# Two-layer hybrid backbone: the short convolution's projections in pieces of six products inside the first segment's attention

## The chip, the cores and the metric

One core of one Trainium2 chip runs the whole program in one launch. The metric is the device time of one execution in microseconds; lower is better. Everything is computed in 32-bit floats and each matrix product is made of three products of high and low halves of its operands.

## What is computed

Two layers over 1024 latent tokens and 256 context tokens of width 1024. In each layer the input projection feeds four groups of heads (a short gated convolution, latent attention, a Conformer convolution module, neighbourhood attention), whose outputs one output projection merges; then comes an MLP. The parts that the change touches:

```
def short_conv_mixer(u_sc, w_sc):
    x_in, b_gate, c_gate = jnp.split(u_sc, 3, axis=-1)
    return b_gate * dwconv(c_gate * x_in, w_sc)

def conformer_conv_mixer(u_cf, w_dw, b_dw, ln_g, ln_b, w_pw):
    a, g = jnp.split(u_cf, 2, axis=-1)
    y = dwconv(a * jax.nn.sigmoid(g), w_dw) + b_dw
    return jax.nn.silu(layernorm(y, ln_g, ln_b)) @ w_pw

def mla_attend(qn, qr, kn, kr, v):
    s = (jnp.einsum("bqhd,bkhd->bhqk", qn, kn)
         + jnp.einsum("bqhr,bkr->bhqk", qr, kr)) * MLA_SCALE
    p = jax.nn.softmax(s.astype(jnp.float32), axis=-1).astype(v.dtype)
    return jnp.einsum("bhqk,bkhd->bqhd", p, v)
```

Neighbourhood attention is the same with a window of keys and a bias for each head, plus all context keys. Context tokens attend to context tokens alone, and the last layer needs no context queries.

## The kernel before

Tokens lie along the columns, in three segments (`SEGS`): 512, 512 and 256 (context) columns; channels lie on the 128 partitions. `mm3` (line 125) makes one output tile: for each of eight channel blocks three products (lines 130 to 132), 24 in all, added up in one PSUM buffer. `inproj` (362) does this for one block of 128 output channels, segment by segment: it loads the weights (two transfers of 256 KB, split into halves `wh` on ACT and `wl` on POOL), draws a buffer `R`, calls `mm3`, hands the buffer to an evacuation and yields a cost of n/100.

PSUM has four kinds of buffers (`ps`, line 91): G (2), S (3), T (2) and O (1). `R` is drawn from a rotation `self.rot`; in the stage of the change it is "G", so that every `R` is a G.

The stage of the change is the attention of segment 0 (`atta` in `layer`, from line 1046): four heads of latent attention (`mla_attend`, 768), each of two blocks of 256 queries, then four heads of neighbourhood attention (`na_attend`, 810), each of two pairs of 128 queries. A tile of 128 latent queries computes its scores against 1280 keys in three S buffers (lines 798 to 800), takes the softmax (`softmax`, 679: maxima on DVE, exponentials with sums on ACT, normalisation on POOL), and after two tiles `pv` (701) transposes the weights two key tiles at a time into T (line 715), splits them and multiplies by the values into O (727, 728); `yput` (731) closes the block with an addition on line 740. Keys, values and the weights share the seven buffers `ah`.

Beside it run two other pieces of work, as generators that `merge` (994) advances: after each yield of `atta` it lets another generator run until its costs reach the attention's costs times its rate (`RATES`). `rest` is the short convolution (`shortconv`, 487): six projections (SCC, SCX, SCB for two channel blocks), over three segments in layer 0 and two in layer 1, 76.8 and 61.4 units of cost; its rate is `ar` (0.392 in layer 0, 0.517 in layer 1). `cfp` is the end of the convolution module (`cf_post`, 447), with rate `ac` (0.6, 0.8): for each segment a mean (products with ones, line 458), a variance, `rstd` (159: sums on line 169, square root on 172, a diagonal product on 178, a copy on 181), a Silu (472) and a pointwise product (481 to 484). The attention has 112 units: 9 a latent block (2, 2, then 5 after `pv`), 5 a neighbourhood pair (1, 1, 3). What is left of the two is emitted after the attention (line 1054).

The order in which a program emits its instructions is their priority, not their order on an engine: a scheduler lays out each engine's order when the program is built, and gives out the buffers of a tag in turn. After the stage come the output projection of segment 0 (`outproj`, 889) and, beside it, the attention of the other segments (`attb`).

Of the kernel before, what the change touches and what calls it, by code (L numbers as in the profile page):

```python
# [12 lines left out]
P = 128  # L13
D = 1024
KT = D // P
LAT = 1024
CTX = 256
TOK = LAT + CTX
# [8 lines left out]
HB = 2  # L27
QTAG = 'xl'
# [4 lines left out]
RATES = dict(pend=(1.0, 1.0), cv=(1.0, 0.862), cp=(1.0, 0.6), hr=(1.0, 0.484), hc=(0.3, 0.3), hm=(0.313, 0.679), ma=(0.195, 0.26), mf=(0.5, 0.5), mv=(0.5, 1.04), cb=(1.0, 1.3), mp=(0.5, 0.5), ar=(0.392, 0.517), ac=(0.6, 0.8), ob=(0.65, 0.696), oc=(0.575, 0.65), od=(0.65, 0.26), on=(0.6, 0.522), mb=(1.0, 0.646), pr=(0.2, 0.2), pt=(0.805, 1.12), pn=(0.612, 1.5), pm=(1.5, 1.5), mn=(1.74, 2.0), mc=(0.29, 0.325), mt=(1.0, 0.6), en=(1.0, 1.0))  # L33
# [36 lines left out]
class Kern:  # L70
# [54 lines left out]
    def mm3(self, out, pairs):  # L125

        nc = self.nc
        last = len(pairs) - 1
        for i, (wh, wl, xh, xl) in enumerate(pairs):
            nc.tensor.matmul(out, wh, xh, start=i == 0, stop=False)  # L130
            nc.tensor.matmul(out, wh, xl, start=False, stop=False)  # L131
            nc.tensor.matmul(out, wl, xh, start=False, stop=i == last)  # L132
# [229 lines left out]
    def inproj(self, l, m, segs, H, evac):  # L362
        wh, wl = self.weights(self.a["win"][l, m], D)
        for si in segs:
            n = SEGS[si][1]
            hi, lo = H[si]
            ps = self.ps("R")[:, :n]
            self.mm3(ps, [(wh(k), wl(k), hi.k(k), lo.k(k)) for k in range(KT)])
            evac(si, ps)
            yield n / 100  # L370
# [76 lines left out]
    def cf_post(self, l, segs):  # L447

        nc = self.nc
        vec = self.vec[:, l]  # L450
        cfy = self.cfy
        wh, wl = self.weights(self.a["wpw"][l], 512)
        for si in segs:
            o, n = SEGS[si]
            cs = [cfy[j][:, o:o + n] for j in range(2)]
            ps = self.ps("R")[:, :n]
            for j in range(2):
                nc.tensor.matmul(ps, self.ones, cs[j], start=j == 0, stop=j == 1)
            yield 4.0
            sqs = []  # L460
# [6 lines left out]
            rs = self.rstd(sqs, 256, n, "G")  # L467
# [12 lines left out]
            for m in range(2):  # L480
                po = self.ps("R")[:, :n]
                self.mm3(po, [(wh(2 * j + m), wl(2 * j + m), zs[j][0], zs[j][1])
                              for j in range(2)])
                nc.scalar.activation(cs[m], po, AF.Copy)
# [216 lines left out]
    def pv(self, ps_list, items, V):  # L701
# [4 lines left out]
        nc = self.nc  # L706
        O = self.ps("O")[:, :2 * P]
        for g in range(0, len(items), 2):
# [15 lines left out]
            for i, (kt, cols) in enumerate(grp):  # L724
                first, last = g + i == 0, g + i == len(items) - 1
                a, b = spans[i]
                nc.tensor.matmul(O[:, a:b], V[:, kt, :], th[:, i, a:b], start=first, stop=False)  # L727
                nc.tensor.matmul(O[:, a:b], V[:, kt, :], tl[:, i, a:b], start=False, stop=last)  # L728
        return O
# [38 lines left out]
    def mla_attend(self, h, segs):  # L768
        nc = self.nc
# [10 lines left out]
        for si in segs:  # L780
            o, n = SEGS[si]
            for q0 in range(0, n, 256):
# [24 lines left out]
                self.yput(self.pv(ps, items, V), 1, h, o + q0)  # L807
                yield 5.0 * L / TOK

    def na_attend(self, l, h, segs):  # L810
# [40 lines left out]
        for si in segs:  # L851
            o, n = SEGS[si]
            for b in range(o // P, (o + n) // P, 2):
# [3 lines left out]
                for bb in (b, b + 1):  # L857
# [24 lines left out]
                    yield 1.0  # L882
                kts = sorted(set(where[0]) | set(where[1]), key=lambda k: (not (k in where[0] and k in where[1]), k))
                items = [(k, tuple(d.get(k) for d in where)) for k in kts]
                self.yput(self.pv(ps, items, V), 3, h, b * P)
                yield 3.0
# [126 lines left out]
    def layer(self, l, H, pend):  # L1013
# [6 lines left out]
        self.rot = ROT0  # L1020
        self.Y, self.Yf, self.cfbuf, self.cfy, self.scy = {}, {}, {}, {}, {}
# [24 lines left out]
        def atta():  # L1046
            for h in range(NH):
                yield from self.mla_attend(h, (0,))
            self.go(rest1)
            for h in range(NH):  # L1050
                yield from self.na_attend(l, h, (0,))

        self.merge(atta(), (rest, R['ar']), (cfp, R['ac']))
        self.go(rest, cfp)
        for m in (1, 2, 0, 3):
            self.ysplit(0, m, "s")
# [288 lines left out]
```

## Time and profile before

| what | us |
|---|---|
| median of 3 runs (lowest, highest) | 3165.7 (3162.52, 3169.48) |
| the profiled execution | 3172.64 |
| its span, first to last instruction | 3170.7 |
| PE busy | 2962.9 |
| DVE, ACT, POOL busy | 1978.2, 1388.2, 1095.1 |
| stage of the change, layer 0 (354 to 608): PE busy | 228.30 of 254 |
| stage of the change, layer 1 (1988 to 2221): PE busy | 209.20 of 233 |

Busy time is the union of an engine's instructions; a matmul's duration includes its way through the array, so that a full PE shows overlapping instructions. PEclk is the granted clock of the PE, 1.00 being 2.4 GHz. A view by stretch gives the busy time of each engine between two times of the span, with the count of instructions in brackets, then PEclk, the mean busy share of the 16 DMA engines and GB/s. PEld is the loading of weights into the PE.

### The profile page before, as it was taken

The page shows a single profiled execution, that of the slowest core. Times are in us where ns is not written, and L with a number is a line of the kernel's source. Part 1 is how long each engine was busy: PE and PEld are TensorE (multiplying, and loading weights), DVE is VectorE, ACT ScalarE, POOL GpSimd, SP SyncE. Part 2 cuts the span into 40 slices and gives each one's busy share as a digit, 9 for nine tenths or more (in the row PEclk, how much of TensorE's full clock was granted, in tenths as well). Part 3 has the DMA queues.
Part 4 walks back from the last instruction along what each step waited for, and adds up shares of the span by engine and source line. Part 5 has one row for each costly group of instructions (what it writes and reads, how often), then busy time and mean ns, then how long its engine had stood idle before and what let it go on. Part 6 is the DMA issues. An engine that isn't in the chain of part 4 may idle for free.

```text
span 3170.7 us, 45433 instructions
## 1 busy us (share of the span) xinstructions
PE 2962.9 (93%) x15720; PEld 2529.0 (80%) x15720; DVE 1978.2 (62%) x3964; ACT 1388.2 (44%) x2840; POOL 1095.1 (35%) x865
## 2 busy tenths in 40 slices
PE   7889889979999989999999998997889999999997
PEld 5777678878888888888888886876878788888886
DVE  8999555686663367566654788556766526344335
ACT  3313445676553355322222533555755434343332
POOL 1302113224544432333332512222324444444443
PEclk9889889989999999999999999998989999999998
DMA  7435423353542263534522534335534324234223
GB/s 265 153 121 190 123 60 104 113 158 100 153 122 97 97 200 100 177 116 168 185 81 80 173 108 165 101 84 138 172 89 148 104 97 143 97 104 139 94 97 103
DMA packets 273193, 405.77 MB, mean 128 GB/s; under 512 B 27074, under 2 KB 124354, under 8 KB 272964
## 3 DMA queue, kind: packets, MB, share of 16 engines
q1 hardware_dynamic: 272964, 402.87, 39.9%
q8 instruction: 125, 2.05, 0.3%
q14 instruction: 104, 0.85, 0.1%
HBM read 350.47 MB, written 52.30 MB: 127 GB/s over the span
## 4 chain that ended last, share of the span: by engine, by line
PE 76%; DVE 5%; DMA 3%; issue 2%; ACT 2%; SPq 1%; POOL 0%; DVEq 0%; ACTq 0%; POOLq 0%
PE G L130 12%; PE G L131 12%; PE G L132 12%; PE S L130 10%; PE S L132 9%; PE S L131 9%; PE T L715 3%; PE O L728 1%; PE O L727 1%; DMA ah<-KR 1%; PE S L849 1%; PE S L799 1%; PE S L798 1%; PE S L800 1%; DVE sm L685 1%
## 5 line engine op out<-in xcount | busy, mean ns | idle before, releaser
L102 POOL TENSOR_TENSOR wl<-raw,wh 128x512 fp32r<-128x512 f32 x676 | 916.4, 1358 | 1479.7 <-ACT wh L101 1358.5
L101 ACT ACTIVATE wh<-raw 128x512 fp32r<-128x512 f32 x752 | 473.0, 631 | 870.2 <-PE S L131 390.9
L130 PE MATMUL G<-h,wh 128*128 128x512 f32 (+1 forms) x1144 | 436.5, 382 | 3.9 <-ACT h L201 1.2
L131 PE MATMUL G<-h,wh 128*128 128x512 f32 (+1 forms) x1144 | 432.4, 378 | 4.4 <-DVE h L202 4.3
L132 PE MATMUL G<-h,wl 128*128 128x512 f32 (+1 forms) x1144 | 432.7, 378 | 0.2 <-POOL wl L102 0.2
L130 PE MATMUL S<-h,wh 128*128 128x512 f32 (+1 forms) x888 | 317.8, 358 | 2.5 <-ACT h L201 1.6
L132 PE MATMUL S<-h,wl 128*128 128x512 f32 (+1 forms) x888 | 316.0, 356 | 1.4 <-POOL wl L102 1.4
L131 PE MATMUL S<-h,wh 128*128 128x512 f32 (+1 forms) x888 | 315.4, 355 | 0.0
L699 POOL TENSOR_SCALAR ah<-ah,sm 128x1280 f32<-128x1280 f32 (+3 forms) x144 | 148.5, 1035 | 407.4 <-DVE sm L698 156.7
L969 DVE TENSOR_TENSOR ac<-ac,S 128x512 f32<-128x512 f32 (+1 forms) x345 | 210.0, 612 | 124.2 <-PE S L132 123.2
L130 PEld LDWEIGHTS G<-h,wh 128*128 128x128 f32 x1144 | 219.5, 192 | 43.3 <-ACT h L201 2.8
L131 PEld LDWEIGHTS G<-h,wh 128*128 128x128 f32 x1144 | 219.5, 192 | 42.9 <-DVE h L202 6.0
L132 PEld LDWEIGHTS G<-h,wl 128*128 128x128 f32 x1144 | 219.4, 192 | 39.0 <-issue 0.7
L102 DVE TENSOR_TENSOR pt<-T,pt 128x512 fp32r<-128x512 f32 (+1 forms) x280 | 169.4, 615 | 90.5 <-ACT pt L101 89.4
L969 DVE TENSOR_TENSOR ac<-ac,G 128x512 f32<-128x512 f32 (+1 forms) x263 | 167.6, 637 | 79.1 <-PE G L132 77.6
L101 ACT ACTIVATE pt<-T 128x512 fp32r<-128x512 f32 (+1 forms) x280 | 146.8, 543 | 117.7 <-PE T L715 104.9
L130 PEld LDWEIGHTS S<-h,wh 128*128 128x128 f32 x888 | 170.8, 192 | 27.9 <-ACT h L201 2.3
L132 PEld LDWEIGHTS S<-h,wl 128*128 128x128 f32 x888 | 170.2, 192 | 27.4 <-POOL wl L102 2.6
L131 PEld LDWEIGHTS S<-h,wh 128*128 128x128 f32 x888 | 170.4, 192 | 24.7 <-issue 0.5
L130 PE MATMUL G<-s,wh 128*128 128x512 f32 (+1 forms) x532 | 184.4, 348 | 2.2 <-ACT ge L903 1.7
L132 PE MATMUL G<-s,wl 128*128 128x512 f32 (+1 forms) x532 | 181.1, 341 | 3.6 <-DVE wl L102 3.5
L131 PE MATMUL G<-s,wh 128*128 128x512 f32 (+1 forms) x532 | 181.6, 342 | 0.3 <-DVE s L102 0.3
(335 smaller groups left out, 6830.6 us busy)
## 6 DMA issues: line engine op xcount, KB each, us to landing
raw<-in_w_dram SPq DMA_DIRECT2D x520, 256.0 KB, 2.5
raw<-in_wout_dram SPq DMA_DIRECT2D x128, 256.0 KB, 3.0
raw<-in_win_dram SPq DMA_DIRECT2D x96, 256.0 KB, 3.0
s<-in_wmodt_dram SPq DMA_DIRECT2D x48, 512.0 KB, 4.2
xl<-in_wmodt_dram SPq DMA_DIRECT2D x64, 256.0 KB, 2.6
ah<-KN SPq DMA_DIRECT2D x32, 320.0 KB, 5.0
ah<-MV SPq DMA_DIRECT2D x16, 640.0 KB, 6.5
ah<-NV SPq DMA_DIRECT2D x16, 640.0 KB, 4.9
```

The costliest lines, as they stand in the source:

```text
L101: nc.scalar.activation(hi, src, AF.Copy)
L102: (eng or nc.vector).tensor_tensor(lo, src, f32(hi), op=ALU.subtract)
L130: nc.tensor.matmul(out, wh, xh, start=i == 0, stop=False)
L131: nc.tensor.matmul(out, wh, xl, start=False, stop=False)
L132: nc.tensor.matmul(out, wl, xh, start=False, stop=i == last)
L685: nc.vector.tensor_reduce(sm[:, i:i + 1], s, op=ALU.max, axis=AX.X)
L699: nc.gpsimd.tensor_scalar(p[:, :L], p[:, :L], sm[:, 9:10], 1.0, op0=ALU.mult, op1=ALU.mult)
L715: nc.tensor.transpose(T[:, i, q * P:(q + 1) * P], ps_list[q][:, cols[q]:cols[q] + P], self.ident)
L727: nc.tensor.matmul(O[:, a:b], V[:, kt, :], th[:, i, a:b], start=first, stop=False)
L728: nc.tensor.matmul(O[:, a:b], V[:, kt, :], tl[:, i, a:b], start=False, stop=last)
L798: nc.tensor.matmul(S, Qt[:, 0, q:q + P], K[0][:, ks], start=True, stop=False)
L969: nc.vector.tensor_tensor(a, a, ps, op=ALU.add)
```

## The change

`mm3` learns to begin and end a sum in separate calls, and `inproj`, while `self.fine` is set, issues its 24 products in four pieces of six (`GRAIN = 2` channel blocks), with a yield of a quarter of the cost after each. `pv` becomes a generator that yields 1.0 after each pair of key tiles, in place of the 5.0 and 3.0 that followed it; the two tiles of a neighbourhood pair yield 2.0 together. The attention's total stays 112 units. The rates become `ar` 0.74 and 0.6, `ac` 0.7 and 0.8. In `cf_post` the mean, `rstd` and the pointwise outputs draw S in place of G, and the first yield of a segment stands ahead of the mean.

```diff
-RATES = dict(... ar=(0.392, 0.517), ac=(0.6, 0.8), ...)
+RATES = dict(... ar=(0.74, 0.6), ac=(0.7, 0.8), ...)
...
-    def mm3(self, out, pairs):
+    def mm3(self, out, pairs, begin=True, end=True):
...
-            nc.tensor.matmul(out, wh, xh, start=i == 0, stop=False)
+            nc.tensor.matmul(out, wh, xh, start=begin and i == 0, stop=False)
             nc.tensor.matmul(out, wh, xl, start=False, stop=False)
-            nc.tensor.matmul(out, wl, xh, start=False, stop=i == last)
+            nc.tensor.matmul(out, wl, xh, start=False, stop=end and i == last)
...
             ps = self.ps("R")[:, :n]
-            self.mm3(ps, [(wh(k), wl(k), hi.k(k), lo.k(k)) for k in range(KT)])
+            pairs = [(wh(k), wl(k), hi.k(k), lo.k(k)) for k in range(KT)]
+            for k in range(0, KT, GRAIN if self.fine else KT):
+                if k:
+                    yield n * GRAIN / (KT * 100)
+                g = GRAIN if self.fine or k else KT
+                self.mm3(ps, pairs[k:k + g], k == 0, k + g == KT)
             evac(si, ps)
-            yield n / 100
+            yield n * g / (KT * 100)
...
-            ps = self.ps("R")[:, :n]
+            yield 4.0
+            ps = self.ps("S")[:, :n]
             for j in range(2):
                 nc.tensor.matmul(ps, self.ones, cs[j], start=j == 0, stop=j == 1)
-            yield 4.0
...
-            rs = self.rstd(sqs, 256, n, "G")
+            rs = self.rstd(sqs, 256, n, "S")
...
-                po = self.ps("R")[:, :n]
+                po = self.ps("S")[:, :n]
...
                 nc.tensor.matmul(O[:, a:b], V[:, kt, :], tl[:, i, a:b], start=False, stop=last)
+            if self.fine:
+                yield 1.0
...
-                self.yput(self.pv(ps, items, V), 1, h, o + q0)
-                yield 5.0 * L / TOK
+                self.yput((yield from self.pv(ps, items, V)), 1, h, o + q0)
+                if not self.fine:
+                    yield 5.0 * L / TOK
...
-                    yield 1.0
+                    if not self.fine:
+                        yield 1.0
+                if self.fine:
+                    yield 2.0
...
-                self.yput(self.pv(ps, items, V), 3, h, b * P)
-                yield 3.0
+                self.yput((yield from self.pv(ps, items, V)), 3, h, b * P)
+                if not self.fine:
+                    yield 3.0
...
+        self.fine = True
         self.merge(atta(), (rest, R['ar']), (cfp, R['ac']))
         self.go(rest, cfp)
+        self.fine = False
```

## Rows read from the trace of the kernel before

**Rows 1.** The page: the span, and each engine's busy time.
```profile
span 3170.7 us, 45433 instructions
...
PE 2962.9 (93%) x15720; PEld 2529.0 (80%) x15720; DVE 1978.2 (62%) x3964; ACT 1388.2 (44%) x2840; POOL 1095.1 (35%) x865
```

**Rows 2.** Layer 0 by stretch: us; PE, PEld, DVE, ACT, POOL busy; PEclk, DMA.
```profile
354.00:428.00 74.00, 70.78 (x395) 59.68 (x393) 41.32 (x95) 41.90 (x92) 18.00 (x13) 0.95 0.24 67
428.00:487.00 59.00, 44.14 (x200) 35.53 (x201) 28.28 (x71) 30.11 (x68) 10.01 (x8) 0.80 0.28 67
487.00:526.00 39.00, 38.87 (x250) 35.00 (x249) 18.71 (x47) 18.98 (x46) 11.63 (x12) 1.00 0.30 86
526.00:567.00 41.00, 40.86 (x246) 36.01 (x245) 31.81 (x73) 24.43 (x55) 12.38 (x14) 1.00 0.43 129
```

**Rows 3.** The same stretches, instructions that read tile h: PE, PEld, DVE, ACT.
```profile
428.00:487.00 59.00, 0.00 (x0) 0.00 (x0) 0.00 (x0) 0.00 (x0) 0.80 0.28 67
487.00:526.00 39.00, 25.94 (x123) 20.01 (x124) 0.00 (x0) 0.00 (x0) 1.00 0.30 86
526.00:567.00 41.00, 29.14 (x135) 21.84 (x134) 0.00 (x0) 0.00 (x0) 1.00 0.43 129
```

**Rows 4.** Instructions in order of time, PE, layer 0: start us, us, what.
```profile
409.34 1.17 PE L169 MATMUL G<-ones,e 128*128 128x1 f32 x10
...
426.99 0.39 PE L131 MATMUL G<-h,wh 128*128 128x512 f32 x1
427.22 0.39 PE L132 MATMUL G<-h,wl 128*128 128x512 f32 x1
...
487.35 0.40 PE L130 MATMUL G<-h,wh 128*128 128x512 f32 x1
```

**Rows 5.** The same view, ACT, the end of the hole.
```profile
468.47 1.28 ACT L172 ACT_TABLE_LOAD   x1
...
475.84 0.68 ACT L692 ACTIVATE ah<-S,sm 128x512 f32<-128x512 f32 x1
...
476.95 0.60 ACT L181 ACTIVATE e<-G 128x512 f32<-128x512 f32 x1
...
486.44 1.09 ACT L484 ACTIVATE c<-G 128x512 f32<-128x512 f32 x2
```

**Rows 6.** Busy time by stretch, layer 1's stage.
```profile
2071.00:2098.00 27.00, 21.35 (x128) 17.24 (x126) 18.16 (x46) 22.93 (x48) 5.40 (x4) 1.00 0.30 71
2098.00:2143.00 45.00, 44.93 (x244) 38.04 (x242) 24.82 (x52) 20.16 (x48) 13.05 (x11) 1.00 0.23 69
2143.00:2180.00 37.00, 29.32 (x173) 27.12 (x174) 28.57 (x68) 23.15 (x54) 8.55 (x12) 0.77 0.59 172
```

**Rows 7.** The same stretches of layer 1, instructions that read tile h.
```profile
2071.00:2098.00 27.00, 0.29 (x1) 0.00 (x0) 0.00 (x0) 0.00 (x0) 1.00 0.30 71
2098.00:2143.00 45.00, 30.75 (x120) 21.75 (x120) 0.00 (x0) 0.00 (x0) 1.00 0.23 69
2143.00:2180.00 37.00, 0.00 (x0) 0.00 (x0) 0.00 (x0) 0.00 (x0) 0.77 0.59 172
```

**Rows 8.** Layer 0 by stretch, the additions of line 740 alone: us, DVE (x).
```profile
428.00:487.00 59.00, 1.65 (x4) 0.80 0.28 67
487.00:526.50 39.50, 0.83 (x2) 1.00 0.30 89
526.50:567.00 40.50, 1.23 (x3) 1.00 0.42 128
567.00:608.00 41.00, 2.09 (x5) 0.85 0.44 121
```

**Rows 9.** Instructions in order of time, a mean of cf_post on PE and DVE.
```profile
356.19 1.88 PE L458 MATMUL G<-c,ones 128*128 128x512 f32 x4
...
358.11 1.29 DVE L462 SCALAR_TENSOR_TENSOR c<-G,c 128x512 f32<-128x512 f32 x2 [2.31 <-PE G L458]
```

**Rows 10.** The chain of waits, a change of head: start us, us, what.
```profile
427.66 5.44 DMA ah<-KR
```

## What the change should do to the time

> **What bounds the kernel now.** I read the page's busy line first: the PE is busy for 2962.9 of 3170.7 us [rows 1]. So time can be won only where the PE idles or runs at half its clock, and the change touches one stage that occurs once in each layer: the attention of segment 0. In layer 0 it runs from the first score product at 354 us to the last output block at 608, in layer 1 from 1988 to 2221. The next view is the busy time by stretch of that stage [rows 2]. The reader is to see three kinds of stretch. From 354 to 428 and from 487 to 567 the PE is full: 38.87 of 39 us and 40.86 of 41 at full clock. From 428 to 487 it is busy for 44.14 of 59 us at a granted clock of 0.80, so two fifths of that time lay at the lower level of 1.2 GHz. What fills the full stretches are the short convolution's projections: the same stretches, asked for the products that read the tile h, show 123 and 135 of them and, in the hole, none [rows 3].
>
> Why none? The tile names and the activation engine's rows tell it. The last projection before the hole is issued at 427.22 and the next at 487.35 [rows 4]. Both kinds of work then take their PSUM from G, which has two buffers. At 409.34 the sums of cf_post's `rstd` are written into a G buffer [rows 4]; the square root that reads them starts with its table load at 468.47, and the copy that frees the buffer ends at 477.55 [rows 5]. The pointwise products come next in the program; their copies end at 487.53 [rows 5], and only then does the next projection get a buffer. Layer 1 has the same hole, shorter: 27 us from 2071 to 2098, PE busy 21.35, one projection product [rows 6, 7].
>
> The third view is the pace of attention, by the additions that close a block of 256 queries (line 740) [rows 8]. In the hole four blocks end in 59 us, 14.8 each, though part of it ran at half clock; in the full stretch of latent attention two in 39.5, 19.8 each. Neighbourhood attention ends three in 40.5 us beside projections, 13.5 each, and five in 41 without, 8.2 each. So attention has a pace of its own, set by its chain of waits, and projections beside it slow it.
>
> **The change part by part.** *The pieces.* A projection is still 24 products, with the same weight loads and flags only at its ends: no instruction is added. A product of 512 columns is issued every 0.23 us (426.99 to 427.22) [rows 4], so a projection is 5.5 us and a piece 1.4. The program's order is not the engine's order: layer 1 emits its last projection when about 109 of the 112 units of attention are emitted (rate 0.517, total 61.4), yet none runs after 2143 [rows 7], ahead of all neighbourhood attention. Projections are pulled forward wherever the PE is free and a buffer is. I therefore price the pieces and the new rates (0.74, 0.6) at nothing by themselves, between -5 us (a delay of up to 5.5 us behind a whole projection becomes 1.4) and +5 (work emitted earlier goes before attention that could run).
>
> *G is left to the projections.* This is the main term. The hole can take its idle time, 14.9 us, and up to half of its 23.6 us at the low clock, 11.8 more: 15 to 27 us, and I take 24, near four and a half projections. They leave the stretch from 487 to 567. That stretch is full, so it falls from 80 us towards 56; attention's own pace sets a floor of 2 x 14.8 + 3 x 8.2 = 54, so the whole 24 can be had. The hole grows in return. By PE time it holds about 34 us of work and then 58; at the loss of the stretch from 354 to 428 (busy 70.78 of 74, clock 0.95, so some 7%) that is 62, or +3. By the pace of blocks beside projections it is 4 x 19.8 = 79, or +20. The sum lies between -21 and -4; I take -13, about the middle: the four blocks were themselves held back by the low clock, which speaks for the PE reading, and the 19.8 is a measured pace, which speaks for the other. In layer 1 the hole's idle time is 5.6 us at full clock, and the stretch after it is full (44.93 of 45) [rows 6]: between -6 and 0, I take -3.
>
> The Trainium skill, Trace Analysis, section Identifying the Most-Contended Engine, says that matmul busy share is a poor measure of how near TensorE is to its limit and wants the share of weight loads instead. The rows bear it out in part: weight loads take 35.00 of 39 us in the full stretch against 35.53 of 59 in the hole [rows 2]. By that rule the full stretch has a tenth in hand, the relief would be 22 us instead of 24, and the sum above -11 instead of -13.
>
> *cf_post moves into S.* S has three buffers, and one tile of 128 queries takes all three (columns 512, 512, 256). A cf_post buffer now stands in that row in the program's order: the tile after it gets its third buffer only when cf_post gives its own back. The holds, from rows: the mean 3.2 us (products at 356.19, last subtraction ends 359.40) [rows 9]; `rstd` 9.1 us (468.47 to 477.55) [rows 5]; the two pointwise outputs 3.9 us (12 products at 0.23, copies 1.09). A buffer would have come back anyhow after the two later exponentials, 1.1 us (475.84 to 476.95, where the copy begins) [rows 5]. So one insertion between two tiles costs up to 2, 8 and 3 us. By the rates, layer 0 emits both `rstd` of its latent attention at a change of head, where the scores wait for keys anyway (5.44 us for the transfer alone) [rows 10]: I price them at nothing there, 8 each if that cover is gone. Its two means and two pointwise steps stand inside a head: 0 to 10 us (the yield of 4.0 that now stands ahead of the mean's buffer keeps it from being held over a merge step; segment 2, of 256 columns, comes in neighbourhood attention, within the same bounds). Layer 1 has one `rstd`, one mean and one pointwise step inside a head: 0 to 13. A head's second block has slack while the next keys are fetched, so I take about a quarter of the two: +6 together.
>
> *What is moved besides.* The weight transfers (two per projection, on SP's queue, past the key and query loads) and their low halves on POOL come earlier: 12 of each in a layer. POOL is busy for 10.01 of 59 us in the hole with 8 instructions [rows 2], so they fit; if one stood ahead of a normalisation each time it would cost its 1.4 us (18.00 us for 13 [rows 2]), 17 us a layer at worst. Price 0. The yields in `pv` and the joint yield of two neighbourhood tiles leave attention's own order as it was: 0. The rotation of S and G in later stages shifts by the 15 buffers that cf_post no longer draws from it: 0, within 3 us either way.
>
> The sum: -13 - 3 + 6 = -10 us. The profiled execution took 3172.6 us (span 3170.7) and would take 3162.6. The median of the runs is 3165.7, 6.9 below the profiled one; I take the difference off the median: 3156.
>
> **The rivals.** *The hole only moves (same, 3163).* Projections are finite. If they run out before neighbourhood attention begins, that part stands bare, as in layer 1: no projection after 2143, PE busy 29.32 of 37 us at clock 0.77 [rows 6, 7]. Then the relief in layer 0 is paid back in the hole at the measured pace (-4), layer 1 gains nothing, and S costs a little: -3 in all. For it: the engine order already pulls projections forward whatever the rates say, so that the pieces do not do what their emission says. Against it: layer 0 has 258 projection products after 487 [rows 3], more than the hole can take.
>
> *S becomes the bound (slower, 3178).* Three buffers are one tile, so every cf_post step in S stops the scores' rotation. If each stands in the chain at full price, the holds cost 10 in layer 0 and 13 in layer 1, and two `rstd` in layer 0 at 8 each when the key transfer has landed before: 39 us. With the holes' gain at its best, -27, that is +12. It decides from where the price of S passes the gain of G: about 16 us, 8 a layer. The Trainium skill, Trace Analysis, section Matmuls, wants independent matmul groups in rotating PSUM banks, so that one is emptied while the next is written; taking banks from the scores goes against that, and by it this rival would hold; no run here has shown it yet. For it, in the rows: `rstd` waited 59 us from its first sums to its square root's table load when it held a G buffer. Against it: inside S, as inside G, buffers go out in the program's order, so the square root cannot be that late there without stopping scores that ScalarE serves next.
>
> *The spread holds (faster, 3142).* If the emission order does keep projections for neighbourhood attention (after 72 of 112 units 53 of 76.8 are emitted in layer 0, 43 of 61.4 in layer 1), both bare ends get work. Layer 1 then moves 18 us out of full stretches into one where the PE idles for 7.7 of 37 us and is at 0.77 of its clock: -14 more at most. Against it: the trace of layer 1, where the order held nothing back.
>
> **How the numbers follow.** Forecast 0.36, the spread 0.12, the hole moves 0.31, S the bound 0.21. A measurement of this kernel can tell about 0.2%, 6 us, from no change. Faster by more: 0.48; within: 0.31; slower: 0.21. The forecast's own range is 3148 (the G term at -21) to 3159 (where no change begins); the range over the cases is 3136 to 3178, from -21 - 6 - 3 to the S rival's +12.
>
> **What would show it.** Right: projection products in the stretch after 428 and after 2071, with the clock near 1 there; layer 0's stage ends near 597 instead of 608; the means, square roots and pointwise outputs named S, with the score tile after each waiting no more than 2 us for its third buffer. Wrong on G: a stretch of over 20 us without projections while some are left. Wrong on S: score products that wait for the copy of line 181 or 484, and a stage of layer 1 longer than 233 us. Rival one: neighbourhood attention without projections in both layers and a stage within 5 us of before. The forecast as a whole is wrong if the stages before 354, between 608 and 1988, or after 2221 change by more than 3 us.

## The result: slower by 0.75%, and the profile after

The changed kernel takes 3193.1 us in the median of five runs (3185.1 to 3199.3), beside 3167.4 for the kernel before (3162.5 to 3174.3): a ratio of 1.0075, with a 95% interval of 1.0063 to 1.0087. That is 24 us slower where 10 us faster was forecast, and outside the range. The profiled execution of after took 3185.1 us and was the shortest of its five, that of before with 3172.6 one of the longer ones, so the two traces show 12.5 us of the difference and the runs tell its size.

The page of after, the lines that answer to [rows 1]:

```profile
span 3183.1 us, 45442 instructions
...
PE 2961.7 (93%) x15720; PEld 2530.7 (80%) x15720; DVE 1977.1 (62%) x3964; ACT 1383.3 (43%) x2836; POOL 1091.8 (34%) x865
```

The PE is busy for as long as before, within 1.2 us; the span is 12.4 us longer. Busy time by stretch of layer 0's stage, the columns of [rows 2], over the same stretches and one more:

```profile
354.00:428.00 74.00, 74.00 (x415) 63.31 (x414) 35.77 (x83) 34.08 (x74) 19.77 (x14) 1.00 0.26 70
428.00:487.00 59.00, 58.17 (x349) 50.57 (x347) 33.90 (x73) 25.35 (x61) 12.65 (x9) 1.00 0.25 63
487.00:526.00 39.00, 29.35 (x150) 23.44 (x150) 20.18 (x52) 24.41 (x54) 8.04 (x8) 0.85 0.31 76
526.00:567.00 41.00, 33.87 (x194) 29.99 (x194) 27.84 (x67) 30.20 (x63) 9.40 (x13) 0.81 0.46 132
567.00:612.00 45.00, 35.06 (x185) 29.07 (x184) 30.64 (x85) 26.76 (x71) 11.07 (x13) 0.85 0.45 118
```

The hole from 428 to 487 is gone: the PE is busy for 58.17 of 59 us at full clock, where [rows 2] had 44.14 at 0.80. But the full stretches behind it are gone too, and the granted clock is at 0.85 and 0.81 where it was 1.00. The products that read the tile h, as in [rows 3]; the first of these lines is of the kernel before, the others of after:

```profile
354.00:428.00 74.00, 32.56 (x151) 24.63 (x151) 0.00 (x0) 0.00 (x0) 0.95 0.24 67
```

```profile
354.00:428.00 74.00, 53.48 (x245) 40.89 (x246) 0.00 (x0) 0.00 (x0) 1.00 0.26 70
428.00:487.00 59.00, 35.84 (x172) 26.83 (x170) 0.00 (x0) 0.00 (x0) 1.00 0.25 63
487.00:526.00 39.00, 0.00 (x0) 0.00 (x0) 0.00 (x0) 0.00 (x0) 0.85 0.31 76
```

Before had run 151 of these products by 487 us, after has run 417, and then none are left. The last one is issued here, beside [rows 4], where projections still begin at 487.35:

```profile
482.96 0.28 PE L133 MATMUL G<-h,wl 128*128 128x256 f32 x1
483.08 0.40 PE L806 MATMUL S<-ah,xl 96*128 96x512 f32 x1
```

Attention paid for it. The additions that close a block, line 748 in after, against [rows 8]; the first of these lines is of the kernel before (line 740), the others of after:

```profile
354.00:428.00 74.00, 0.81 (x2) 0.95 0.24 67
```

```profile
354.00:428.00 74.00, 0.82 (x2) 1.00 0.26 70
428.00:487.00 59.00, 0.84 (x2) 1.00 0.25 63
487.00:526.50 39.50, 1.25 (x3) 0.84 0.31 77
526.50:567.00 40.50, 1.40 (x4) 0.81 0.46 132
567.00:612.00 45.00, 2.33 (x6) 0.85 0.45 118
```

Two blocks end in the former hole instead of four (one addition lies across 567 us and is counted in both of the last two lines). By 487 us the PE has done more than before (132.2 us busy at clock 1.00, instead of 114.9 at 0.95 and 0.80), but in projections, and the twelve blocks still open must end by themselves. What the PE waits for while they do, from 487 to 567:

```profile
PE T L721 <- POOL ah L705: 7.3, 4, 4.2
PE O L734 <- DVE sm L695: 2.0, 3, 1.0
PE O L734 <- DVE pt L103: 1.7, 4, 0.8
PE O L733 <- ACT pt L102: 1.6, 2, 1.1
```

(columns: us in total, times, the longest; these are the four largest of ten entries, 17.2 us together). These are attention's own steps: the weights of the softmax before they are transposed, its sums, the halves of the transposed weights. From 354 to 487 the same view has one wait of 0.3 us, and in before it has none at all from 487 to 567. Layer 1 repeats it, its products on h in after, as in [rows 7]:

```profile
2050.00:2079.00 29.00, 21.75 (x85) 15.27 (x85) 0.00 (x0) 0.00 (x0) 1.00 0.11 35
2079.00:2106.00 27.00, 14.07 (x57) 10.36 (x57) 0.00 (x0) 0.00 (x0) 1.00 0.39 101
2106.00:2151.00 45.00, 0.00 (x0) 0.00 (x0) 0.00 (x0) 0.00 (x0) 0.85 0.24 57
```

The last product on h in the stage ends at 2103 us instead of 2141. Lengths by section of the program, from one profiled execution each, read off the first score products, and off the 16th, 40th and 56th closing additions:

```
                     stage of  rest of L0's  to first   stage of  to the   span
                     layer 0   attention     score, L1  layer 1   end
before                251.6      323.1        1060.0     230.8    951.2   3170.7
e16_heads_turn        245.1      324.2        1060.8     235.4    945.0   3166.1
e7_rot_shift          248.1      331.1        1064.1     234.1    944.6   3175.6
e11_nudged            244.3      325.5        1057.2     225.2    951.9   3158.5
e10_shadow_S          237.9      326.1        1059.6     245.3    944.2   3168.5
e15_shadow_L0         238.2      326.6        1059.3     226.3    952.6   3161.5
e5_only_rates         247.0      328.8        1059.1     241.1    947.4   3177.5
e2_cf_in_G            244.2      328.5        1058.8     244.2    943.6   3175.4
e9_one_G              252.6      324.5        1057.9     238.9    944.4   3171.4
e8_S_rot_kept         256.8      328.9        1058.7     240.7    945.5   3188.7
e3_only_S             253.9      335.9        1067.6     234.3    943.4   3188.4
e6_rot_kept           254.6      324.2        1058.1     240.0    949.6   3182.3
e13_all_one_G         256.8      327.8        1057.8     239.4    952.4   3192.0
e14_heads_back        254.9      329.0        1060.8     239.0    942.0   3179.7
e4_whole              254.9      330.7        1070.6     234.9    943.7   3189.1
after                 254.8      329.2        1066.0     237.0    941.9   3183.1
e1_old_rates          258.6      332.7        1069.3     233.9    944.3   3192.3
e12_pinned            257.9      322.4        1057.5     235.0    955.6   3177.9
```

The first three rows have the same order of PE instructions through layer 0's stage, yet it takes 251.6, 245.1 and 248.1 us: one trace's stage is good to some 3 us either way, and their mean is 248.3. After and the three kernels with its order of PE instructions in this stage (e4_whole, e14_heads_back, e6_rot_kept) give 254.6 to 254.9. So layer 0's stage lost about 6.5 us; two traces alone, 251.6 against 254.8, would have shown half of it.

### The profile page after: what moved, and what is told of

It is laid out like the page before. It is cut to its first block, busy times and chain, and to the rows that moved or that the text cites. A ratio compares the mean times of both kernels' runs of the same rounds, so it can differ in the third digit from the quotient of the medians.

```text
span 3183.1 us, 45442 instructions
## 1 busy us (share of the span) xinstructions
PE 2961.7 (93%) x15720; PEld 2530.7 (80%) x15720; DVE 1977.1 (62%) x3964; ACT 1383.3 (43%) x2836; POOL 1091.8 (34%) x865
## 5 line engine op out<-in xcount | busy, mean ns | idle before, releaser
L131 PE MATMUL G<-h,wh 128*128 128x512 f32 (+1 forms) x1080 | 398.6, 369 | 3.9 <-ACT e L554 1.1
L132 PE MATMUL G<-h,wh 128*128 128x512 f32 (+1 forms) x1080 | 397.7, 368 | 4.3 <-DVE h L203 4.3
L133 PE MATMUL G<-h,wl 128*128 128x512 f32 (+1 forms) x1080 | 396.6, 367 | 0.0
L131 PE MATMUL S<-h,wh 128*128 128x512 f32 (+1 forms) x952 | 351.7, 371 | 3.9 <-ACT h L202 2.7
L133 PE MATMUL S<-h,wl 128*128 128x512 f32 (+1 forms) x952 | 350.8, 369 | 1.4 <-POOL wl L103 1.4
L132 PE MATMUL S<-h,wh 128*128 128x512 f32 (+1 forms) x952 | 350.8, 369 | 0.0
L131 PEld LDWEIGHTS G<-h,wh 128*128 128x128 f32 x1080 | 207.5, 192 | 37.3 <-ACT e L554 1.4
L132 PEld LDWEIGHTS G<-h,wh 128*128 128x128 f32 x1080 | 207.2, 192 | 37.2 <-DVE h L203 5.7
L133 PEld LDWEIGHTS G<-h,wl 128*128 128x128 f32 x1080 | 207.0, 192 | 31.8 <-issue 1.0
L131 PEld LDWEIGHTS S<-h,wh 128*128 128x128 f32 x952 | 182.8, 193 | 35.1 <-ACT h L202 3.8
L133 PEld LDWEIGHTS S<-h,wl 128*128 128x128 f32 x952 | 182.4, 192 | 32.9 <-POOL wl L103 2.2
L132 PEld LDWEIGHTS S<-h,wh 128*128 128x128 f32 x952 | 182.8, 192 | 30.0 <-issue 0.5
L952 DVE TENSOR_TENSOR S<-S,ge 128x512 f32<-128x512 f32 (+1 forms) x84 | 52.7, 627 | 225.0 <-ACT ge L948 224.7
L131 PE MATMUL G<-s,wh 128*128 128x512 f32 (+1 forms) x530 | 184.4, 350 | 4.0 <-ACT ge L916 2.5
```

The costliest lines, as they stand in the source:

```text
L131: nc.tensor.matmul(out, wh, xh, start=begin and i == 0, stop=False)
L133: nc.tensor.matmul(out, wl, xh, start=False, stop=end and i == last)
L952: nc.vector.tensor_tensor(ps, ps, r, op=ALU.mult)
```

## The experiments

**Which part costs: the pieces and the rates.**

```diff
# e4_whole: after, with
-GRAIN = 2
+GRAIN = 8
# e5_only_rates: before, with
-ar=(0.392, 0.517), ac=(0.6, 0.8)
+ar=(0.74, 0.6), ac=(0.7, 0.8)
# e1_old_rates: after, with the rates of before
```

> The changed kernel with projections emitted whole (eight channel blocks to a piece), the yields of pv kept. Theory pieces: the time changes by more than 8 us. Theory stock: within 6 us of the changed kernel, since the products of a projection are spread among attention's by the scheduler in either form (in the trace of before a projection is cut by scores as well).

> The kernel before with the new rates alone (ar 0.74 and 0.6, ac 0.7 and 0.8), projections whole, cf_post in G. Theory stock: slower than before by 8 to 25 us, projections end earlier than in before (567 and 2141 us). Theories S and pieces: within 6 us of before.

> The changed kernel with the rates of before (ar 0.392 and 0.517, ac 0.6 and 0.8); pieces and S stay. Theory stock (the higher rates emit projections ahead of attention, so the PE is full of them until 483 and 2105 us and attention stands bare at a clock near 0.85 for the rest): projections last past 510 in layer 0 and past 2125 in layer 1, and the time falls by 10 to 25 us from the changed kernel, to 3165 to 3180. Theory S (cf_post in the scores' buffers is what delays attention): the time stays within 6 us of the changed kernel's, 3187 to 3199. Theory pieces (the finer yields themselves): within 6 us as well.

With whole projections the time is 3191.3 us (1.0082, 1.0065 to 1.0099), after's own 1.0075. The pieces cost and bring nothing: in the two traces the PE takes its 15720 products in the same order, buffer numbers apart. The new rates alone make before slower, 3178.7 (1.0041, 1.0028 to 1.0055), and in its trace layer 1's stage is longer, 241.1 us. Taken off after they don't give that back, 3199.7 (1.0106, 1.0086 to 1.0127): projections ended at 484.7 and 2112 us there too, so where cf_post is in S the rates no longer decide when projections run.

**Which part costs: cf_post in S, and the turn of the two tags.** Outside the stage, draws of the tag R take S and G by turns (S, G, S, G, S). Cf_post draws nine times in layer 0 and six in layer 1, so after has the turn shifted by one place (nine draws of a cycle of five) from layer 0's stage to layer 1's, and in its old place again behind that.

```diff
# e2_cf_in_G: after, with cf_post's four draws back in R, G, R
# e3_only_S: before, with
+            yield 4.0
-            ps = self.ps("R")[:, :n]
+            ps = self.ps("S")[:, :n]
...
-            yield 4.0
...
-            rs = self.rstd(sqs, 256, n, "G")
+            rs = self.rstd(sqs, 256, n, "S")
...
-                po = self.ps("R")[:, :n]
+                po = self.ps("S")[:, :n]
# e7_rot_shift: before, with "self.rcount -= 1" at each R draw of cf_post
# e6_rot_kept: after, with "self.rcount += 1" at the same places
# e8_S_rot_kept: e3_only_S, with that too
```

> The changed kernel with cf_post's PSUM back in G (mean, rstd, pointwise). Theory S: 10 to 25 us faster than the changed kernel. Theory stock: holes without projections come back, which stretches the stock, while the high rates still put the rest ahead of attention: between 0 and 12 us faster, projections end later than 483 and 2105 us. Theory pieces: within 6 us of the changed kernel.

> The kernel before with cf_post's PSUM in S and its yield moved, nothing else. Theory S: 10 to 25 us slower than before. Theory stock: within 8 us of before, because with the old rates projections keep a lower priority than attention; the hole of layer 0 between 428 and 487 is gone and projections end before 567. My forecast's own mechanism (G left to projections is a gain of some 10 us) asks for 3150 to 3160 here.

> The kernel before with the rotation counter taken back after each of cf_post's draws: cf_post still uses G, but later stages have the shifted turn of the changed kernel. Theory rotation: 6 to 16 us slower than before, lost outside the stage. Theory stock: within 5 us of before.

> The changed kernel with the rotation counter advanced wherever cf_post draws an S buffer, so that all later stages draw S and G in the same turn as in the kernel before. Theory rotation (the shifted turn of S and G costs time outside the stage: 6 us between 608 and 942, the end of the other segments' attention): 6 to 16 us faster than the changed kernel, and the gaps to before at the end of layer 0's attention within 4 us. Theory stock (projections run out early): within 5 us of the changed kernel's 3187 to 3199.

> The kernel before with cf_post in S and the rotation kept. It differs from the third experiment by the rotation alone and from before by S alone. Theory rotation: within 10 us of before. Theory stock, or S as such: 15 to 30 us slower than before, most of it in layer 1 between 1988 and 2241.

Measured: cf_post back in G, 3176.1 us (1.0028, 1.0013 to 1.0042); cf_post in S alone, 3196.4 (1.0099, 1.0076 to 1.0122); the shift alone, 3183.0 (1.0055, 1.0038 to 1.0072); after without the shift, 3184.9 (1.0061, 1.0046 to 1.0076); in S without the shift, 3190.2 (1.0071, 1.0056 to 1.0087). So the move into S costs: with cf_post back in G after is 15 us faster (0.0047 of 3166), and on before the move alone costs 31 us, more than any of my cases had. Both pairs change the turn along with the move. With the turn kept on both sides the move costs 22 us on before (e8) and 10 on the new rates and pieces (e6 against e2). The shift by itself costs 17 us, more than the 6 to 16 that I gave it; on top of the move it costs 4 to 9, with intervals that meet. The parts don't add up; the lengths by section show where, in the part on the prediction.

With cf_post back in G the hole returns in part, and with it the late projections. Products on h in that kernel:

```profile
354.00:428.00 74.00, 41.21 (x194) 31.00 (x192) 0.00 (x0) 0.00 (x0) 1.00 0.22 64
428.00:487.00 59.00, 18.19 (x87) 14.08 (x88) 0.00 (x0) 0.00 (x0) 0.91 0.33 80
487.00:526.00 39.00, 25.48 (x114) 18.90 (x112) 0.00 (x0) 0.00 (x0) 1.00 0.28 83
```

The PE is less full there than in after, and the stage is shorter, 244.2 us.

**Is it the lost S buffer?** The kernels e10 and e15 leave cf_post in G, and take a buffer of S beside each of its steps for as long as the step holds its own.

```diff
# e10_shadow_S: before, with (and likewise at rstd and at the two outputs)
             ps = self.ps("R")[:, :n]
+            sh = self.ps("S")
+            nc.vector.memset(sh[:, 0:1], 0.0)
...
+            nc.vector.tensor_copy(sh[:, 0:1], cs[1][:, 0:1])
# e15_shadow_L0: the same under "if l == 0"
```

> The kernel before, cf_post's results still in G, but each of its steps also draws an S buffer, touches one column of it at its start and its end, and gives it back with the G buffer: the scores lose the buffer as in the changed kernel, while G is as crowded as before. Theory S: 10 to 25 us slower than before. Theory crowding: within 6 us of before.

> Before, with a buffer of S held beside each step of cf_post as in the shadow kernel, in layer 0 alone. Its trace showed layer 0's stage 14 us shorter and layer 1's 14 longer. If both are real, layer 0 alone gives 3154 (3150 to 3160). If they are what one execution differs from the next, it is 3166 (3161 to 3170).

3168.2 us (1.0006, 0.9993 to 1.0019), and in layer 0 alone 3166.9 (1.0008, 1.0 to 1.0017). The S buffer held beside cf_post costs nothing by the runs. But the order changes with it, and the projections are not where they were in before; products on h in e10:

```profile
428.00:487.00 59.00, 13.78 (x64) 10.40 (x64) 0.00 (x0) 0.00 (x0) 1.00 0.20 52
```

The last of them ends at 578 us, where before's ends at 569. So e10 shows that S can be shared at no cost beside this order, not beside the order that after has. The hope behind e15, that e10's shorter stage in layer 0 (237.9 us) was a gain hidden by a loss in layer 1, fell: the stage is as short again, 238.2, and the time is not. What takes the gain back is not found.

**Is it that projections have both G buffers?** One buffer of G is held from the stage's start to its end.

```diff
# e9_one_G: e8_S_rot_kept, and e13_all_one_G: e6_rot_kept, each with
+        held = self.ps("G")
+        self.nc.vector.memset(held[:, 0:1], 0.0)
         self.merge(atta(), (rest, R['ar']), (cfp, R['ac']))
         self.go(rest, cfp)
+        self.nc.vector.memset(held[:, 0:1], 0.0)
```

> The kernel of the eighth experiment (before, cf_post in S, rotation kept; 3190 us) with one of the two G buffers held unused from the start of the stage to its end, so that projections have a single buffer, as they had in the holes of before. Theory crowding (G freed lets projections fill the PE without a gap; attention is slowed while they last and stands bare after they run out): projections last at least 20 us longer than 484 and 2112 us, and the time falls by 8 to 20 us, to 3170 to 3182. Theory S (cf_post among the scores delays attention): no gain, 3184 to 3200.

> After, with the turn of S and G kept and one G buffer held for the whole stage. If the pieces, the yields and the new rates cost nothing once the projections have one G buffer, the time is that of the kernel with cf_post alone in S and one G buffer, 3172 (3168 to 3178). If the new rates cost their own 12 us here too, it is 3184 (3180 to 3190). Projections end near 483 in layer 0 either way.

The first, 3172.6 us (1.0021, 1.0008 to 1.0034), took off 16 of e8's 22 us and seemed to settle it. The second, 3191.5 (1.0085, 1.007 to 1.01), took off nothing. And the trace of the first shows that the cause it was built for did not act. Its products on h:

```profile
354.00:428.00 74.00, 52.43 (x239) 39.05 (x237) 0.00 (x0) 0.00 (x0) 1.00 0.22 62
428.00:487.00 59.00, 36.71 (x179) 28.55 (x179) 0.00 (x0) 0.00 (x0) 1.00 0.30 76
487.00:526.00 39.00, 0.00 (x0) 0.00 (x0) 0.00 (x0) 0.00 (x0) 0.87 0.27 79
```

With one buffer the projections run out at the same time as with two. The second buffer is not what lets them crowd in; cf_post's absence from their queue is enough. Why e9 is 16 us faster than e8 stays open: in the table the difference is spread over all five columns, none with more than 4.4 us of it, and 5 us more lie ahead of the stage.

**Does it help to spread them?** The first product of each piece is pinned to its place in the program's order, so that it can't be pulled ahead of attention.

```diff
# e12_pinned: e6_rot_kept, with, in mm3
+            ins = nc.tensor.matmul(out, wh, xh, start=begin and i == 0, stop=False)
+            if pin and i == 0:
+                self.pin(ins)
```

> The changed kernel with the rotation kept and the first product of each piece pinned behind all PE work emitted before it, so that projections keep the places that the rates give them. Theory crowding: projections reach into neighbourhood attention in both layers (products that read h after 526 and after 2152 us), attention is not slowed early, and the time falls below the sixth experiment's 3185, to 3150 to 3178. If instead PE stalls behind pinned pieces whose weights or buffer are late, over 3190.

3179.5 us (1.0041, 1.0025 to 1.0058). The pins did hold projections back, 81 products from 526 to 567 us and 46 behind that, and the clock was 0.947 over the stage instead of 0.920. The stage was still 257.9 us long, though it begins with the first score at 349.6 us, some 3 us or more ahead of all others (352.9 to 358.5), and so holds some more work. The time is between my two cases. A pinned product that waits for its buffer holds all behind it, so the trial is not clean: the higher clock at the stage's end bought no time here, and whether a cleaner spread would is not shown.

**Is there free room at the end?** Two more projections in each layer behind the last, 49.7 us of products together, whose results go nowhere.

```diff
# e17_more_after: after, and e18_more_before: before, each with, in shortconv
+        for j in range(2):
+            yield from self.inproj(l, M_SCB + j, segs, H, nul)
+        self.rcount -= 2 * len(segs)
```

> After, with two more projections in each layer behind the last, over the same segments; their results go nowhere. That is 27.6 us of products in layer 0 and 22.1 in layer 1 (0.23 us each), 49.7 together. If the bare end that the early projections leave has room for them, they are nearly free in after: 3193 + 0 to 15, 3193 to 3208, and after is then within 10 us of before with the same addition. If attention slows beside projections by what these take, there is no free room at the end either: 3193 + 35 to 60, 3228 to 3253.

> Before, with the same two more projections in each layer, 49.7 us of products. Its projections already reach to 571 us in layer 0, 36 us ahead of the stage's end. If room at the end decides, before has less of it than after and pays more: 3166 + 25 to 45, 3191 to 3211. If attention slows beside projections by what these take, it pays what after pays, 3201 to 3226, and the distance of the two kernels stays.

After went to 3223.7 us (1.018, 1.0163 to 1.0197), 31 more in the median than without; before to 3189.9 (1.0072, 1.0056 to 1.0088), 24 more. Neither of my two cases: half of the 49.7 us is free in before, and two fifths in after, whose bare end I had thought the emptier. The place tells why. Products on h in the enlarged before, and then in the enlarged after:

```profile
567.00:612.00 45.00, 30.39 (x142) 22.47 (x140) 0.00 (x0) 0.00 (x0) 1.00 0.40 109
```

```profile
487.00:526.00 39.00, 22.68 (x100) 16.80 (x99) 0.00 (x0) 0.00 (x0) 1.00 0.33 83
526.00:567.00 41.00, 9.79 (x48) 7.13 (x46) 0.00 (x0) 0.00 (x0) 0.96 0.42 121
567.00:612.00 45.00, 0.00 (x0) 0.00 (x0) 0.00 (x0) 0.00 (x0) 0.73 0.55 151
```

In before the addition lies beside neighbourhood attention and lengthens the stage to 255.0 us, 3.4 more than before's trace and 6.7 more than the mean, for 27.6 us of products. In after it runs as soon as the others are done, beside latent attention, and lengthens the stage by 10.4, to 265.2; the end stays bare. Room at the end is there, and projections that run as early as they can don't reach it.

**The turn, alone and undone, at one place.**

```diff
# e14_heads_back: after, with
+        self.rcount += 9 * l
         self.merge(heads, (rest1, R['hr']), (conv, R['hc']), (moda, R['hm']))
+        self.rcount -= 9 * l
# e16_heads_turn: before, with l in the place of 9 * l
```

> After, with the turn of S and G set back to that of before for the heads' stage of layer 1 alone (nine draws added ahead of it and taken off behind it); the rest is after's. If the shifted turn costs where it meets that stage, the stretch from the transposes of the latent keys to the first score product falls from 122 to 113 us, and the time from 3193 to 3185 (3180 to 3188). If the cost is one of the whole order, the stretch stays near 122 and the time near 3193.

> Before, with the turn of S and G moved one draw on for the heads' stage of layer 1 alone and moved back behind it, as after has it there. By the theory that the shifted turn costs where it meets that stage, the stretch from the transposes to the first score product grows from 114 to 122 us and the time to 3174 (3170 to 3180), about half of what the shift alone cost. If the turn by itself costs nothing there, 3166 (3161 to 3169).

Undoing the shift for layer 1's heads gives 3189.7 us (1.0076, 1.0062 to 1.009), no change by the ratio; the stretch from the transposes to the first score fell from 121.8 to 116.6 us, not to 113. Doing it there alone gives 3172.2 (1.0029, 1.0016 to 1.0042), as expected in time but not in place: that stretch was 115.4. So only a part of the shift's 17 us comes from the heads. Nor is that stretch the same work in both turns: with the shifted turn (after, e7, e16) one projection of 24 products, 5.5 us, runs ahead of the first score, and 264 products on h are left for the stage instead of 288. In the table the shift's mark is in two columns: the opening of layer 1 is 1064 to 1071 us in the kernels that carry the shift throughout, and 1057 to 1061 in all others; the rest of layer 0's attention is 329 to 336 against 322 to 329.

**A control.** Before, with rates moved by a twentieth.

```diff
# e11_nudged: before, with
-ar=(0.392, 0.517)
+ar=(0.41, 0.535)
```

> The kernel before with the rate of the short convolution nudged from 0.392 and 0.517 to 0.41 and 0.535; nothing else. Theory tuned order (the order of before sits at the good end of what the scheduler gives, and any change of emission order or of the turn of buffers costs some 5 to 17 us, as the shifted rotation and the new rates did): 4 to 15 us slower than before. Without that theory: within 4 us, since a projection moves by at most one step of attention.

3164.3 us (0.9997, 0.9983 to 1.001). This disturbance of the order costs nothing. It is a weak control: the PE order changes in layer 0's attention alone, and from there on it is before's, while the edits above reach the later stages.

## Why the prediction was wrong, step by step

**The reading of the bound was right as far as it went.** The hole was cf_post's. In S the square root of `rstd` no longer waits; after's second one in the stage, the counterpart of the one in [rows 5]:

```profile
488.19 1.95 PE L170 MATMUL S<-ones,e 128*128 128x1 f32 x16 [0.33 <-ACT ah L698]
490.21 1.28 ACT L173 ACT_TABLE_LOAD   x1 [0.55 <-PE S L170]
...
495.66 0.60 ACT L182 ACTIVATE e<-S 128x512 f32<-128x512 f32 x1 [1.11 <-PE S L179]
```

From the table load to the end of the copy it holds its buffer for 6.1 us (the other two of the stage 8.7 and 7.1), where I had put 9.1. But a G buffer held by `rstd` does not make a hole by itself. Before's third `rstd` holds one from 500.79 to 565.03 us, nearly as long as the second, and in that time projections run with no pause of over 2 us. Its first sums and its last copy, and the products on h between them, all in before:

```profile
500.79 0.95 PE L169 MATMUL G<-ones,e 128*128 128x1 f32 x8
564.65 0.38 ACT L181 ACTIVATE e<-G 128x256 f32<-128x256 f32 x1
```

```profile
500.70:565.00 64.30, 43.95 (x195) 32.36 (x193) 0.00 (x0) 0.00 (x0) 1.00 0.40 119
```

In the hole the other G buffer lay empty from 428.3, where the last projection's is read out, to 481.4, where the first pointwise product is written. Both had to be out of reach at once: one held by `rstd`, the other, as I read the order of the program, already given to the pointwise outputs that stand next. No view shows whom an empty buffer is kept for, but e9 and e13 fit: there one held G buffer, with cf_post out of the queue, does not stop projections.

**The step that failed is the main term, "G is left to the projections": -13 us in layer 0, where the stage came out 6.5 us longer.** Its first half came true: the hole's idle time and low clock were won, and by 487 us the PE was ahead. The failure is in two assumptions behind it. One: that the relief is the hole's size, 24 us or 104 products, and leaves the rest of the order alone. In fact 266 products came forward, 94 of them into the stretch from 354 to 428, which I had called full and left out; there they displaced attention. Two: the floor of 54 us for what follows 487 took it that four blocks would close in the hole as before. Two did. With four latent and eight neighbourhood blocks open, the same paces, 14.8 and 8.2, give a floor of 4 x 14.8 + 8 x 8.2 = 125 us; from 487 to the stage's end at 609.0 it took 122. I had the right prices and the wrong count of blocks. The pace for the hole, 19.8 at worst, was also too low: two blocks in 59 us are 29.5 each.

The low clock tells it in one number. Over layer 0's stage the mean granted clock is 0.919 in before and 0.920 in after: the low stretch was moved from the hole to the end, not removed.

**The first rival named this and priced it wrongly.** "The hole only moves" said that projections could run out before neighbourhood attention begins, and spoke of it as -3 us. They ran out even before the latent blocks were done. What I held against it, 258 products left after 487, was a count from an order that the change itself would undo. Price: layer 0's stage takes 6.5 us more (254.8 against 248.3). Layer 1's takes 6 more (237.0 against 230.8), and the last column gives 9 back.

**The second step that failed: the rotation was priced at 0, within 3 us, and costs 17 alone.** I took a shifted buffer turn for a matter of names. It decides which draws stand behind which, and two stages with no edit in them became longer. That the shift is 15 draws was counted rightly, and 15 is three whole cycles; but between the layers it stands at nine. My own sign for an error, stages outside the change that move by more than 3 us, is met: from the end of layer 0's stage to the first score of layer 1 it is 12.1 us longer.

The lengths by section divide the loss, if each section is averaged over those kernels of the table whose traces have the same order of PE instructions in it. Against before (0 where the order is before's):

```
                              stage of  rest of L0's  to first   stage of  to the  sum   by the
                              layer 0   attention     score, L1  layer 1   end           runs
after, turn kept (e6)           +6.5       +0.7          0         +12.0      0     +19    +19
the shift alone (e7)             0         +7.4        +7.8         +6.7    -6.5    +15    +17
after                           +6.5       +6.0        +9.4         +7.0    -7.5    +21    +24
```

An entry is good to some 3 us, and the sums come near to what the runs say. Of after's loss 6.5 us lie in the stage in which projections run out; 15 lie between its end and layer 1's first score, where the shift alone loses as much. The parts fail to add in layer 1: with the turn kept its stage is 12 us longer (the new rates alone, e5, do as much there, 241.1), with the shifted turn its stage and what follows lose nothing together. Why the turn decides that is not known.

**S as the bound has no support.** That goes for the term of +6 and the rival's +12: e10 pays 1.0006. The Trainium skill, Perfetto Trace Analysis, section Matmuls, wants independent matmul groups to rotate through different PSUM banks, and I read that as speaking for this rival. After's trace does not bear it out: while projections filled the PE it never waited for an S buffer (its one wait from 354 to 487, of 0.3 us, is for O). Of my two signs, scores that wait for cf_post's copies stand nowhere in after's two stages. A stage of layer 1 over 233 us is there (237.0), but the shift alone, with cf_post in G, gives 234.1. A kernel that frees G without taking S was not run, so that a lost S buffer costs beside after's order is not excluded. This rival had the right sign, and its mechanism is not seen.

**The rates were priced at 0, within 5, and cost 13 on before**; the pieces at 0 were right.

**The spread** was forecast to gain most. The kernel that spreads, e12, gains nothing over e6 that its intervals can tell (1.0041 against 1.0061), with the reservation above.

What is shown: the move of cf_post into S costs (10 to 22 us with the turn kept), and so does the shifted turn; where cf_post is in S and the scheduler orders the same projections freely, they run out at 483 to 498 us and attention stands alone behind them. That the move's loss in layer 0 comes from the freed queue and not from S is argued, from e10 and from the order of the stages: layer 0's takes 253 to 259 us where projections end at 483 to 498 (cf_post in S), 244 to 252 where they end at 549 to 569 (in G), and 238 where they end at 578 and 582 (e10 and e15), leaving out the kernel with pins and the two with added projections. What is not settled: why the shifted turn lengthens the sections that it does, and why e9 escaped.

## What to carry to other kernels

Work that fills the gaps of a latency-bound chain is a finite stock: before freeing its queue, count how much of it is left behind the gap and what the chain will look like when it is gone, in blocks still open and not in idle microseconds. Filling a hole is a gain only if the filler came from a place that can spare it. And a change in how many buffers a step draws from a rotation is an edit to every later stage, to be measured by itself or cancelled.

## What the runs showed of the chip that was not expected

A full PE is no sign of progress: from 354 to 487 us after's PE is busy for 132.2 of 133 us at full clock, and closes four blocks where before, busy for 114.9 with a lower clock, closes six. And the same order of PE instructions can differ by 6.5 us in one stage of 250 (251.6, 248.1, 245.1), the clock over it being 0.919, 0.931 and 0.944: differences of a few microseconds between two traces are read from several kernels or not at all.
